# Score tiles by head instead of by residue: stacked high and low queries in the attention of a two-layer trunk

## The chip, the cores and the metric

The kernel runs on one core of a Trainium2 chip. The metric is the time of one execution on the device in microseconds (us); lower is better. Five engines matter: TensorE (PE; its weight loads are listed as PEld), VectorE (DVE), ScalarE (ACT), GpSimd (POOL) and SyncE (SP), which here issues the DMA loads.

## What is computed

A trunk of two layers for 256 tokens of width 1024: a mixture of three dilated causal attentions, a gated convolutional channel mixer, a gated linear attention, and the channel mixer again. The change is in the first of these. Cut to what matters:

```python
A_CONFIGS = ((128, 1), (512, 4), (2048, 16))     # window, dilation of groups 0, 1, 2

def dilated_branch(q, k, v, table, window, dilation):
    # query t attends t - j*dilation, j = 0..window/dilation, with a T5 bias
    ...
    s = jnp.einsum('bnqrhe,bnkrhe->bnrhqk', qb, kk).astype(jnp.float32) + bias[None, None, None]
    s = jnp.where(mask[None, :, None, None], s, NEG_INF)
    m = jnp.max(s, axis=-1, keepdims=True)
    p = jnp.exp(s - m)
    den = jnp.sum(p, axis=-1)
    o = jnp.einsum('bnrhqk,bnkrhe->bnqrhe', p, vv.astype(jnp.float32))
    ...

def dilated_mixture(h, w_in, w_out, rel_bias):
    qkv = (h @ w_in).reshape(B, S, A_GROUPS, 3, A_HEADS, A_HEAD_DIM)
    ...                                   # one branch for each group, joined by a softmax over their lse
    return o.reshape(B, S, A_WIDTH).astype(h.dtype) @ w_out
```

There are 16 heads of 64 channels. Because the branches are joined by a softmax of their log-sums, the kernel puts a query's scores of all three groups into one row and takes a single softmax over it: 256 scores of group 0 (dilation 1), and 64 each of groups 1 and 2, since with 256 tokens a query sees only keys of its own residue modulo 4 there (group 2's dilation of 16 is a mask within that residue).

## The kernel before

**Number format.** Most products are made of parts: a float32 value is split into a high part in a format of fewer bits that TensorE takes in one pass (`F32R`) and the rest, the low part, and `mm3` adds high·high, high·low and low·high. Plain `F32` products take several passes. Weights come in over SP in chunks of up to 2048 columns (`split`: tile `raw`, four buffers), ScalarE makes the high part `whi` (L172) and VectorE the low part `wlo` (L178), three buffers each.

**The attention loop** (L626) runs over eight pairs of heads; a pair fills the 128 partitions, head 0 in rows 0 to 63, head 1 in 64 to 127. For pair `u` it projects queries and keys of the groups 0, 1, 2 (`pqk`; three weight loads `wqk`), then values (`pv`; two loads `wv`, in the two rounds of `half`), then makes the scores (`scores`, L476) and the outputs of the pair before (`outputs`, L550). The turning of a pair's probabilities by TensorE (`turn`, L536) lies in the middle of the next pair's projections (L671, L678). Pairs 0 and 1 are projected together, from the first weights `w0` (L640 to L657). Six half chunks of the adaLN weights are loaded and multiplied in each pair from 2 on (`next_half`, L457).

**Evacuation** (`evacuate`, L576) of group 0: ScalarE writes the high part of the scaled queries (L586), VectorE their low part (L587), for each head; then ScalarE the high part of the keys and VectorE the low one (L591). The query tiles are zero where a row belongs to the other head: `q[0][a][:, r]` is, for a residue `r`, 128 rows by 2 x 64 columns with only the two diagonal blocks filled. GpSimd writes these zeros once, before the loop (L614).

**Score tiles.** There are four for a pair, one for each residue `r` modulo 4, 64 queries of head 0 in rows 0 to 63 and 64 of head 1 in rows 64 to 127. `shared` (L485) makes three products of 128 rows and 256 to 260 columns for each tile; `dilated` (L494) makes the small ones, 64 x 64 x 64 in plain `F32`: two groups by two heads for each tile. VectorE then adds the bias and takes the maximum (L510), with each query's bias row read backwards from tile `bias`; ScalarE takes the exponential (L529); VectorE divides by the sum and brings the keys into order by residue (`normalised`, L521 and L522).

**Bias rows.** `load_bias` (L364) fetches one tile for a pair with four DMAs from a small table in DRAM (`rows_d`), two buffers. In the loop it stands ahead of the pair's weight loads (L627).

**Order.** A scheduler puts each engine's instructions in a fixed order at compile time, by program order and its own model of time; an instruction that waits holds up everything behind it on its engine or queue. `tc.issue_after(x)` and the helper `behind(x)` only place an instruction after `x` on its engine. `behind(last_pv)` puts score products behind the last value product; the first tile's may come earlier (L503). PSUM tiles come from `bank`, with 2, 3 and 3 buffers of the tags p, s and t.

Of the kernel before, what the change touches and what calls it, by code (L numbers as in the profile page):

```python
# [18 lines left out]
P = 128  # L19
# [38 lines left out]
def trunk(ctx: ExitStack, tc: tile.TileContext, I, out):  # L58
# [305 lines left out]
    def load_bias(u):  # L364

        b = att.tile([P, KEYS + 3], F32, tag="bias", name="bias")
        r = rows_d[:, :]
        for hh in range(2):  # L370
            own, at = slice(CH * hh, CH * hh + CH), r.offset + (2 * u + hh) * NROW
            nc.sync.dma_start(b[own, 2 * CH :], bass.AP(r.tensor, at, [[4, CH], [1, T + 3]]))
            nc.sync.dma_start(b[own, 0 : 2 * CH].rearrange("p (g x) -> p g x", g=2),
                              bass.AP(r.tensor, at + 512, [[1, CH], [P, 2], [1, CH]]))
        return b[:, :]
# [100 lines left out]
    def scores(u, q, k, v, bias):  # L476
# [3 lines left out]
        prob = [att.tile([P, KEYS + 3], F32, tag="prob", name="prob", bufs=4) for _ in range(4)]  # L480

        def shared(s, r):
            n = T + r + r % 2
            for i, (a, b) in enumerate(((0, 0), (1, 0), (0, 1))):
                last = mm(s[:, 0:n], q[0][a][:, r].rearrange("p a b -> p (a b)"), k[0][b][:, 0:n], start=(i == 0), stop=(i == 2))  # L485
            return last

        def dilated(s, r):
            own = slice(CH * r, CH * r + CH)
            for g in (1, 2):  # L490
                at = T + r + CH * (g - 1)
                for hh in range(2):
                    e = slice(E * hh, E * hh + E)
                    last = mm(s[e, at : at + CH], q[g][e, own], k[g][e, own], start=True, stop=True)  # L494
            return last
# [3 lines left out]
        for tiles in ((0, 1, 2), (3,)) if u == 0 else (range(4),):  # L499
            s = {r: bank("s", "t" if r == 3 and u else "s") for r in tiles}  # L500
            for r in tiles:

                with behind(*(last_pv if r else last_t if u > 2 else [])):  # L503
                    last = shared(s[r], r)
            for r in tiles:
                with behind(last):
                    last = last_s[0] = dilated(s[r], r)
            for r in tiles:
# [41 lines left out]
    def outputs(u, of, pt, *after):  # L550
# [3 lines left out]
        with behind(*after):  # L554
            for n in range(2):
                for hh, e in enumerate(heads):
                    mm(grouped(po[e, :T]), v[n][:, e], pt[:, :, P * n + E * hh : P * n + E * hh + E], start=(n == 0), stop=False)
# [738 lines left out]
```

## Time and profile before

| | |
|---|---|
| runs | 769.24, 769.94, 769.95 us; median 769.94 |
| span of the profiled execution | 767.7 us; its time from outside is not shown |
| mean granted TensorE clock | 0.998 |
| HBM read | 182.59 MB, 239 GB/s over the span |
| `shared`, L485 | 96 products, 277 to 389 ns each by the trace |
| `dilated`, L494 | 128 products in 256 passes, 218 to 267 ns each by the trace |
| bias, maximum, L510 | 32 instructions, 546 to 561 ns each |
| bias loads, L372 and L373 | 32 DMAs, 450 to 1350 ns of SP each |

The profile is that of one execution. Times within it are us from the start of its span. Products overlap in the array, so how long one is said to take is more than what it adds; the distance from one start to the next tells that. In the rows of a timeline stand: start, duration, engine, line, operation, output<-inputs, tile shape and how many were merged; in brackets how long the engine idled before and who ended that.

### The profile page before, as it was taken

The page shows a single profiled execution, that of the slowest core. Times are in us where ns is not written, and L with a number is a line of the kernel's source. Part 1 is how long each engine was busy: PE and PEld are TensorE (multiplying, and loading weights), DVE is VectorE, ACT ScalarE, POOL GpSimd, SP SyncE. Part 2 cuts the span into 40 slices and gives each one's busy share as a digit, 9 for nine tenths or more (in the row PEclk, how much of TensorE's full clock was granted, in tenths as well). Part 3 has the DMA queues.
Part 4 walks back from the last instruction along what each step waited for, and adds up shares of the span by engine and source line. Part 5 has one row for each costly group of instructions (what it writes and reads, how often), then busy time and mean ns, then how long its engine had stood idle before and what let it go on. Part 6 is the DMA issues. An engine that isn't in the chain of part 4 may idle for free.

```text
span 767.7 us, 15963 instructions
## 1 busy us (share of the span) xinstructions
PE 759.3 (99%) x6430; PEld 739.0 (96%) x6430; DVE 640.6 (83%) x1160; ACT 485.5 (63%) x949; POOL 13.2 (2%) x28
## 2 busy tenths in 40 slices
PE   8999999999999999999999999999999999999997
PEld 6999999999999999999999998899999999999996
DVE  6998988888888869999999778797668899998552
ACT  6477566465646568776767556745767866666552
POOL 1000000000000010000000000000010000000100
PEclk9999999999999999999999999999999999999999
DMA  8989778787787347878646975875355777644531
GB/s 346 402 298 408 269 244 278 255 277 261 278 275 245 112 146 279 333 239 272 235 139 234 353 277 202 328 257 189 131 192 196 251 267 256 239 151 152 192 110 56
DMA packets 35208, 184.72 MB, mean 241 GB/s; under 512 B 6140, under 2 KB 7676, under 8 KB 21182
## 3 DMA queue, kind: packets, MB, share of 16 engines
q1 hardware_dynamic: 34752, 183.26, 67.7%
q8 instruction: 50, 0.82, 0.4%
q10 hardware_dynamic: 382, 0.45, 0.2%
q14 instruction: 24, 0.20, 0.1%
HBM read 182.59 MB, written 1.10 MB: 239 GB/s over the span
## 4 chain that ended last, share of the span: by engine, by line
PE 93%; DMA 3%; ACT 2%; DVE 2%; issue 0%; ACTq 0%
PE pab L200 10%; PE pab L199 10%; PE pab L201 10%; PE pqk L199 5%; PE pqk L201 5%; PE pqk L200 5%; PE pd L200 5%; PE pd L199 5%; PE pd L201 5%; PE pv L200 3%; PE pv L199 3%; PE pv L201 3%; DMA raw<-in_w 2%; PE py L199 2%; PE py L201 2%; PE py L200 2%
## 5 line engine op out<-in xcount | busy, mean ns | idle before, releaser
L172 ACT CAST whi<-raw 128x1024 fp32r<-128x1024 f32 (+4 forms) x270 | 243.7, 946 | 104.0 <-PE pab L200 37.2
L178 DVE TENSOR_TENSOR wlo<-raw,whi 128x1024 fp32r<-128x1024 f32 (+3 forms) x254 | 270.5, 1091 | 44.0 <-ACT whi L172 43.3
L200 PE MATMUL pab<-hlo,whi 128*128 128x256 f32 x672 | 184.6, 276 | 0.0
L201 PE MATMUL pab<-hhi,wlo 128*128 128x256 f32 x672 | 184.6, 276 | 0.0
L199 PE MATMUL pab<-hhi,whi 128*128 128x256 f32 x672 | 183.2, 277 | 0.0
L200 PEld LDWEIGHTS pab<-hlo,whi 128*128 128x128 f32 x672 | 126.0, 188 | 0.2
L201 PEld LDWEIGHTS pab<-hhi,wlo 128*128 128x128 f32 x672 | 126.1, 188 | 0.0
L199 PEld LDWEIGHTS pab<-hhi,whi 128*128 128x128 f32 x672 | 125.1, 188 | 0.1
L140 DVE CUSTOM_DVE_ANT_0 ada_raw<-ada_raw,c_bc 128x1024 f32<-128x1024 f32 x96 | 113.0, 1218 | 5.7 <-DMA ada_raw<-in_w_ada 4.2
L199 PE MATMUL pqk<-hhi,whi 128*128 128x256 f32 x356 | 98.0, 281 | 0.0
L200 PE MATMUL pqk<-hlo,whi 128*128 128x256 f32 x356 | 97.4, 279 | 0.0
L201 PE MATMUL pd<-ghi,wlo 128*128 128x256 f32 x352 | 96.9, 276 | 0.0
L200 PE MATMUL pd<-glo,whi 128*128 128x256 f32 x352 | 96.9, 276 | 0.0
L199 PE MATMUL pd<-ghi,whi 128*128 128x256 f32 x352 | 96.8, 276 | 0.0
L201 PE MATMUL pqk<-hhi,wlo 128*128 128x256 f32 x356 | 96.7, 279 | 0.0
L199 PEld LDWEIGHTS pqk<-hhi,whi 128*128 128x128 f32 x356 | 66.5, 188 | 0.2
L200 PEld LDWEIGHTS pqk<-hlo,whi 128*128 128x128 f32 x356 | 66.7, 188 | 0.0
L201 PEld LDWEIGHTS pqk<-hhi,wlo 128*128 128x128 f32 x356 | 65.9, 188 | 0.7 <-issue 0.7
L200 PEld LDWEIGHTS pd<-glo,whi 128*128 128x128 f32 x352 | 66.0, 188 | 0.0
L201 PEld LDWEIGHTS pd<-ghi,wlo 128*128 128x128 f32 x352 | 66.0, 188 | 0.0
L199 PEld LDWEIGHTS pd<-ghi,whi 128*128 128x128 f32 x352 | 65.9, 188 | 0.0
L852 ACT ACTIVATE r<-pab,small 128x256 f32<-128x256 f32 x86 | 47.4, 559 | 7.3 <-DVE r L855 6.9
(248 smaller groups left out, 1408.8 us busy)
## 6 DMA issues: line engine op xcount, KB each, us to landing
raw<-in_w_up SPq DMA_DIRECT2D x42, 1024.0 KB, 4.9
ada_raw<-in_w_ada SPq DMA_DIRECT2D x29, 1024.0 KB, 5.9
raw<-in_w_down SPq DMA_DIRECT2D x32, 704.0 KB, 4.1
ada_raw<-in_w_ada SPq DMA_DIRECT2D x38, 512.0 KB, 6.4
raw<-in_wqk SPq DMA_DIRECT2D x18, 1024.0 KB, 5.9
raw<-in_wv SPq DMA_DIRECT2D x14, 768.0 KB, 5.9
raw<-in_w SPq DMA_DIRECT2D x7, 960.0 KB, 6.4
raw<-in_w_out_a SPq DMA_DIRECT2D x4, 1024.0 KB, 6.6
```

What stands on the lines that cost most here:

```text
L140: i = nc.vector.tensor_tensor_reduce(w, w, c_bc, op0=ALU.mult, op1=ALU.add, scale=1.0, scalar=0.0, accum_out=dot,)
L172: copied[0] = nc.scalar.copy(hi[:, c], raw[:, c])
L178: last_lo[0] = nc.vector.tensor_tensor(lo[:, c], raw[:, c], hi[:, c].bitcast(F32), op=ALU.subtract)
L199: mm(ps, a[0], b[0], start=start, stop=False)
L200: mm(ps, a[0], b[1], start=False, stop=False)
L201: return mm(ps, a[1], b[0], start=False, stop=stop)
L852: nc.scalar.activation(r, u[:, :T], AF.Identity, scale=cw[2], bias=col(C_CB + 44 * l + f))
```

## The change

- A score tile now holds 128 queries of one head: tile `i` belongs to head `i % 2` and to the residues `2 * (i // 2)` and the next one, one above the other.
- The query tile `qs` holds for each head the high part in the head's own 64 rows and the low part in the other 64. The key tile `ks` holds for each head the high part of its keys in both halves. One product of 128 rows gives high·high + low·high (`shared`), one of the head's 64 rows gives high·low (`rest_of`): two for each tile instead of three.
- The products of a pair are ordered: those of 128 rows for all tiles, those of 64 rows, then the small ones. These go, for each half of the tiles and each group, through (head, residue) = (0,0), (1,1), (0,1), (1,0).
- In `evacuate` ScalarE writes both queries and the keys `kh` first, VectorE the low parts after, and GpSimd copies `kh` into `ks`, four copies of 64 x 256.
- Each head has its own bias tile, four DMAs each, so eight for a pair; single-buffered from pair 1 on (pair 0's stand in a tile of `pt`). From pair 2 on they are issued after the first value load of the pair.
- The zeros in the query tiles are no longer written. The outputs read the probabilities in the new layout. The first tile's products, too, come after the value products from pair 2 on.

The core of the diff:

```diff
@@ -363,16 +363,20 @@
     def load_bias(u):
-
-
-        b = att.tile([P, KEYS + 3], F32, tag="bias", name="bias")
+        both = []
         r = rows_d[:, :]
+        first = None if u else att.tile([P, 4, KEYS], F32, tag="pt", name="bias")
         for hh in range(2):
-            own, at = slice(CH * hh, CH * hh + CH), r.offset + (2 * u + hh) * NROW
-            nc.sync.dma_start(b[own, 2 * CH :], bass.AP(r.tensor, at, [[4, CH], [1, T + 3]]))
-            nc.sync.dma_start(b[own, 0 : 2 * CH].rearrange("p (g x) -> p g x", g=2),
-                              bass.AP(r.tensor, at + 512, [[1, CH], [P, 2], [1, CH]]))
-        return b[:, :]
+            b = (first[:, 2 * hh : 2 * hh + 2, :].rearrange("p a b -> p (a b)")[:, 0 : KEYS + 2] if u == 0
+                 else att.tile([P, KEYS + 2], F32, tag=f"bias{hh}", name="bias", bufs=1)[:, :])
+            at = r.offset + (2 * u + hh) * NROW
+            for x in range(2):
+                own = slice(CH * x, CH * x + CH)
+                nc.sync.dma_start(b[own, 2 * CH :], bass.AP(r.tensor, at + x, [[4, CH], [1, T + 2]]))
+                nc.sync.dma_start(b[own, 0 : 2 * CH].rearrange("p (g x) -> p g x", g=2),
+                                  bass.AP(r.tensor, at + 512, [[1, CH], [P, 2], [1, CH]]))
+            both.append(b)
+        return both
     sq = wspl.tile([P, 2048], F32, tag="wlo", name="sq").rearrange("p (k t) -> p k t", k=KT)
@@ -478,38 +482,51 @@
         m = tmp.tile([P, 16], F32, tag="m", name="m")
         prob = [att.tile([P, KEYS + 3], F32, tag="prob", name="prob", bufs=4) for _ in range(4)]
-
-        def shared(s, r):
-            n = T + r + r % 2
-            for i, (a, b) in enumerate(((0, 0), (1, 0), (0, 1))):
-                last = mm(s[:, 0:n], q[0][a][:, r].rearrange("p a b -> p (a b)"), k[0][b][:, 0:n], start=(i == 0), stop=(i == 2))
+        qs, (ks, kl) = q[0], k[0]
+
+        def width(i):
+            return T + 2 * (i // 2)
+
+        def shared(s, i):
+            hh, n = i % 2, width(i)
+            return mm(s[:, 0:n], qs[:, hh, P * (i // 2) : P * (i // 2) + P], ks[:, T * hh : T * hh + n], start=True, stop=False)
+
+        def rest_of(s, i):
+            hh, n = i % 2, width(i)
+            e = slice(E * hh, E * hh + E)
+            return mm(s[:, 0:n], qs[e, hh, P * (i // 2) : P * (i // 2) + P], kl[e, 0:n], start=False, stop=True)
+
+        def dilated(s, tiles):
+            for half in range(2):
+                for g in (1, 2):
+                    for hh, x in ((0, 0), (1, 1), (0, 1), (1, 0)):
+                        i = 2 * half + hh
+                        if i in tiles:
+                            e, own = slice(E * hh, E * hh + E), slice(CH * (2 * half + x), CH * (2 * half + x) + CH)
+                            at = width(i) + CH * (g - 1)
+                            last = mm(s[i][CH * x : CH * x + CH, at : at + CH], q[g][e, own], k[g][e, own], start=True, stop=True)
             return last
-        def dilated(s, r):
-            own = slice(CH * r, CH * r + CH)
-            for g in (1, 2):
-                at = T + r + CH * (g - 1)
-                for hh in range(2):
-                    e = slice(E * hh, E * hh + E)
-                    last = mm(s[e, at : at + CH], q[g][e, own], k[g][e, own], start=True, stop=True)
-            return last
-
         for tiles in ((0, 1, 2), (3,)) if u == 0 else (range(4),):
-            s = {r: bank("s", "t" if r == 3 and u else "s") for r in tiles}
-            for r in tiles:
-
-                with behind(*(last_pv if r else last_t if u > 2 else [])):
-                    last = shared(s[r], r)
-            for r in tiles:
+            s = {i: bank("s", "t" if i == 3 and u else "s") for i in tiles}
+            for i in tiles:
+                with behind(*(last_pv if i or u > 1 else [])):
+                    last = shared(s[i], i)
+            for i in tiles:
                 with behind(last):
-                    last = last_s[0] = dilated(s[r], r)
-            for r in tiles:
-                back = bass.AP(bias.tensor, bias.offset + KEYS - 1 + r, [bias.ap[0], [-1, KEYS + r]])
+                    ends = rest_of(s[i], i)
+            last = ends
+            with behind(last):
+                last_s[0] = dilated(s, tiles)
+            for i in tiles:
+                n = KEYS + 2 * (i // 2)
+                b = bias[i % 2]
+                back = bass.AP(b.tensor, b.offset + n - 1, [b.ap[0], [-1, n]])
                 nc.vector.tensor_tensor_reduce(
-                    prob[r][:, 0 : KEYS + r], s[r][:, 0 : KEYS + r], back,
-                    op0=ALU.add, op1=ALU.max, scale=1.0, scalar=-3e38, accum_out=m[:, r : r + 1],
+                    prob[i][:, 0:n], s[i][:, 0:n], back,
+                    op0=ALU.add, op1=ALU.max, scale=1.0, scalar=-3e38, accum_out=m[:, i : i + 1],
                 )
         pn = []
@@ -519,13 +536,13 @@
             f = m[:, 12 + r : 13 + r]
             pn.append(att.tile([P, KEYS], F32, tag="pn", name="pn", bufs=4))
             nc.vector.tensor_scalar(grouped(pn[r][:, 0:T]), by_residue(prob[r][:, 0:T]), f, None, op0=ALU.mult)
-            norms.append(nc.vector.tensor_scalar(pn[r][:, T:KEYS], prob[r][:, T + r : KEYS + r], f, None, op0=ALU.mult))
+            norms.append(nc.vector.tensor_scalar(pn[r][:, T:KEYS], prob[r][:, width(r) : KEYS + width(r) - T], f, None, op0=ALU.mult))
         for hh in range(2):
             rs = slice(2 * hh, 2 * hh + 2)
             nc.vector.tensor_scalar(m[:, 4:8][:, rs], m[:, 0:4][:, rs], -1.0, None, op0=ALU.mult)
             for r in (2 * hh, 2 * hh + 1):
-                c = prob[r][:, 0 : KEYS + r]
+                c = prob[r][:, 0 : KEYS + width(r) - T]
                 exps.append(nc.scalar.activation(c, c, AF.Exp, bias=m[:, 4 + r : 5 + r], accum_out=m[:, 8 + r : 9 + r]))
             nc.vector.reciprocal(m[:, 12:16][:, rs], m[:, 8:12][:, rs])
             for r in (2 * hh, 2 * hh + 1):
@@ -554,12 +571,12 @@
         with behind(*after):
             for n in range(2):
                 for hh, e in enumerate(heads):
-                    mm(grouped(po[e, :T]), v[n][:, e], pt[:, :, P * n + E * hh : P * n + E * hh + E], start=(n == 0), stop=False)
+                    mm(po[e, :T].rearrange("p (a b) -> p a b", a=2), v[n][:, e], pt[:, hh::2, P * n : P * n + P], start=(n == 0), stop=False)
             for r in range(4):
                 for hh, e in enumerate(heads):
                     at = P * (r % 2) + P + E * hh
                     last_po[0] = mm(po[e, CH * r : CH * r + CH], v[r // 2][:, at : at + E],
-                       pt[:, r, T + E * hh : T + E * hh + E], start=False, stop=(r == 3))
+                       pt[:, 2 * (r // 2) + hh, T + CH * (r % 2) : T + CH * (r % 2) + CH], start=False, stop=(r == 3))
         if u == 0:
             shift(att, 8)
         hi = att.tile([P, T], F32R, tag=f"ohi{u}", name="ohi", bufs=1)
@@ -580,16 +597,21 @@
         if g:
             evacuated[:] = nc.scalar.mul(q[g], pq, 0.125), nc.vector.tensor_copy(k[g], pk)
             return evacuated[1]
-        qh, ql = q[0]
-        for hh in range(2):
-            own = slice(E * hh, E * hh + E)
-            nc.scalar.mul(qh[own, :, hh, :], grouped(pq[own]), 0.125)
-            nc.vector.scalar_tensor_tensor(ql[own, :, hh, :], grouped(pq[own]), 0.125, qh[own, :, hh, :].bitcast(F32),
+        qs, (ks, kl, kh) = q[0], k[0]
+        k[0] = ks, kl
+        heads = [slice(E * hh, E * hh + E) for hh in range(2)]
+        for hh, own in enumerate(heads):
+            nc.scalar.mul(qs[own, hh, :], pq[own], 0.125)
+        high = nc.scalar.copy(as_tokens(kh[:, 0:T]), in_order(pk))
+        for hh, own in enumerate(heads):
+            nc.vector.scalar_tensor_tensor(qs[heads[1 - hh], hh, :], pq[own], 0.125, qs[own, hh, :].bitcast(F32),
                                            op0=ALU.mult, op1=ALU.subtract)
-        pk = in_order(pk)
-        kh, kl = (as_tokens(z[:, 0:T]) for z in k[0])
-        evacuated[:] = nc.scalar.copy(kh, pk), nc.vector.tensor_tensor(kl, pk, kh.bitcast(F32), op=ALU.subtract)
-        return evacuated[1]
+        low = nc.vector.tensor_tensor(as_tokens(kl[:, 0:T]), in_order(pk), as_tokens(kh[:, 0:T]).bitcast(F32), op=ALU.subtract)
+        for hh, own in enumerate(heads):
+            for to in heads:
+                nc.gpsimd.tensor_copy(ks[to, T * hh : T * hh + T], kh[own, 0:T])
+        evacuated[:] = high, low
+        return low
     def by_group(v, pv, n):
@@ -609,10 +631,11 @@
     for i in range(2):
         q_pair.append([])
         for j in range(2):
-            at, n = ((112, 2 * T + 112), (0, 2 * T + 16))[j] if i == 0 else (0, 2 * T)
+            at, n = ((112, 2 * T + 112), (0, 2 * T + 16))[j] if i == 0 else (0, 2 * T + 8 * j)
             z = att.tile([P, n], F32R, tag=f"q0{i}{j}", name="q", bufs=1)
-            nc.gpsimd.memset(z.bitcast(F32), 0.0)
-            q_pair[i].append(z[:, at : at + 2 * T].rearrange("p (r h c) -> p r h c", r=4, h=2))
+            if j:
+                nc.gpsimd.memset(z[:, 2 * T :].bitcast(F32), 0.0)
+            q_pair[i].append(z[:, at:] if j else z[:, at : at + 2 * T].rearrange("p (h c) -> p h c", h=2))
             if i == 0:
                 for s in range(2):
                     level[s].append(z[:, at + T * s : at + T * s + T])
@@ -624,14 +647,15 @@
                     nc.scalar.copy(a, b)
     for u in range(NPAIR):
-        with tc.issue_after(last_load[0].ins):
-            bias = load_bias(u)
+        if u < 2:
+            with tc.issue_after(last_load[0].ins):
+                bias = load_bias(u)
         place = u % 2 if u < 4 else 1
         if u == 0:
-            k_hi, k_lo = ([att.tile([P, T + 4], F32R, tag=f"k0{i}{j}", name="k", bufs=1) for j in range(2)] for i in range(2))
-            for z in k_hi + k_lo:
+            k_hi, k_lo = ([att.tile([P, T + 4 * (i or j)], F32R, tag=f"k0{i}{j}", name="k", bufs=1) for j in range(2)] for i in range(2))
+            for z in k_lo:
                 nc.gpsimd.memset(z[:, T:].bitcast(F32), 0.0)
-        q, k = [q_pair[place]], [[k_hi[place], k_lo[place]]]
+        q, k = [q_pair[place][0]], [(q_pair[place][1], k_lo[place], k_hi[place])]
         for g in (1, 2):
             q.append(att.tile([P, T], F32, tag=f"q{g}", name="q"))
             k.append(att.tile([P, T], F32, tag=f"k{g}", name="k"))
@@ -699,6 +723,9 @@
                     else:
                         hi = lo = ()
                     w = split(I["wv"][u - 1, half], 1536, after=(hi, ()), low=lo)
+                if u > 1 and half == 0:
+                    with tc.issue_after(last_load[0].ins):
+                        bias = load_bias(u)
                 for k4 in range(4):
                     kt = 4 * half + k4
                     wv = parts(w, 384 * k4, 384)
```

## The prediction

> **What bounds the kernel now.** I read the page's totals first, then the busy times over one period of the attention loop (the pairs repeat every 30.36 us; this row runs from the score products of pair 4 to those of pair 5), then TensorE's instructions in order of time.
>
> ```profile
> span 767.7 us, 15963 instructions
> PE 759.3 (99%) x6430; PEld 739.0 (96%) x6430; DVE 640.6 (83%) x1160; ACT 485.5 (63%) x949; POOL 13.2 (2%) x28
> ...
> 161.71:192.07 30.36, 30.36 (x273) 29.80 (x273) 26.09 (x53) 17.79 (x42) 0.00 (x0) 1.00 0.77 262
> ```
>
> In that row the length is followed by the busy time of PE, PEld, DVE, ACT and POOL, then the granted clock and the DMA share. TensorE is busy in every one of the 30.36 us, at full clock; VectorE has 4.3 us to spare, ScalarE 12.6, GpSimd is empty. So a pair lasts as long as its products, and what counts is when each group of them starts, not how long one is called busy (281 ns, while one starts every 118).
>
> ```profile
> 147.42 0.48 PE L485 MATMUL s<-k,q 128*128 128x256 f32 x2
> 147.75 0.28 PE L199 MATMUL pqk<-q,whi 128*128 128x256 f32 x1
> ...
> 153.27 0.28 PE L485 MATMUL s<-k,q 128*128 128x256 f32 x1
> 153.39 0.34 PE L199 MATMUL pv<-whi,hhi 128*128 128x384 f32 x1
> ...
> 161.71 1.24 PE L485 MATMUL s<-k,q 128*128 128x258 f32 x9
> 162.88 1.15 PE L494 MATMUL s<-k,q 64*64 64x64 f32 x32
> 163.96 1.08 PE L557 MATMUL po<-pt,v 128*64 128x256 f32 x8
> 164.87 0.64 PE L561 MATMUL po<-pt,v 128*64 128x64 f32 x16
> 165.43 0.39 PE L199 MATMUL pqk<-q,whi 128*128 128x256 f32 x1
> ```
>
> The twelve `shared` products of a pair are three early ones, used as fillers, and nine in a row. One costs 153.39 - 153.27 = 0.12 us (0.118 below, the spacing inside the nine); 9 x 0.118 = 1.06 of the 1.17 us to the first small product, so the change of tile shape costs 0.10. The 16 small products are float32 and show as 32 passes, in 1.08 us.
>
> How much runs side by side is read from these rows:
>
> ```profile
> 283.89 2.76 PE L329 MATMUL early<-early_x,raw 128*128 128x257 f32 x12
> 286.30 0.58 PE L199 MATMUL pab<-hhi,whi 128*128 128x256 f32 x2
> ...
> 507.11 0.28 PE L200 MATMUL pqk<-hlo,whi 128*128 128x256 f32 x1
> 507.32 0.48 PE L1040 MATMUL kv<-v,kdT 64*128 64x256 f32 x1
> 507.32 0.48 PE L1040 MATMUL kdt<-v,kdT 64*128 64x256 f32 x1
> 507.64 0.38 PE L1040 MATMUL kv<-v,kdT 64*128 64x256 f32 x1
> ...
> 507.85 0.59 PE L1040 MATMUL kv<-v,kdT 64*128 64x256 f32 x2
> 508.38 0.39 PE L201 MATMUL pqk<-hhi,wlo 128*128 128x256 f32 x1
> ```
>
> On the whole array twelve float32 passes of 257 columns take 2.41 us, 0.20 each. L557 has passes of the same length, yet eight of them take 0.91 us to L561: its two heads, in the two column halves of the array, run together. L1040 shows the same for row halves: `kv` and `kdt`, 64 rows each, start in the same instant, while the third product, on rows already used, takes its two passes alone (507.85 to 508.38). The small products run two at a time as well: 64 columns are a quarter of a pass, 0.05 us, and 32 of those one after the other would be 1.6 us, not 1.08. Two is what their order allows: each head has one quadrant of the array, rows and columns of its own half. L1040 also prices entering the 64-row shape: 0.21 from the last start before (0.10 above the usual 0.118), and 0.32 instead of 0.21 for the first pass, whose weights nothing hides: 0.10 + 0.10. For weights of 64 columns I take half of that, 0.05; of the 1.08 us then 0.05 is first weights, 0.10 the shape change out, and 0.93 the 16 slots, 0.058 each.
>
> **The change, part by part.** *Score products.* Four of 128 rows replace eight (high and low queries stacked, one high key under both), and four of 64 rows replace the other four. Tiles alternate heads, so the 64-row ones use alternate row halves and run in two slots, as L1040's did. Per pair, before: 12 x 0.118 + 0.10 (into 64x64) + 0.05 (first weights) + 0.93 + 0.10 (out) = 2.60. After: 4 x 0.118 = 0.47; 0.10 + 0.10 into 64 rows; 2 x 0.118 = 0.24; 0.10 + 0.05 into 64x64; the small ones; 0.10 out: 1.16 plus the small ones. If the 64-row products did not overlap: 0.24 more.
>
> *Small products.* Their count and size stay, but four in succession now lie in four different quadrants, two banks. No row of before has four at once. Bounds: 0.93 us (two at a time, as now) and 0.47 (8 slots). Column halves together (L557) and row halves together (L1040) both stand in the trace, so I take 0.47. The pair then costs 1.63 and saves 0.97; at 0.93 it saves 0.51. Pair 0 runs tiles 0 to 2 and then 3 apart, pays the extra shape change twice and has lone tiles with only two quadrants: by the same prices 0.43 saved (0.19 with two at a time). Sum: 7 x 0.97 + 0.43 = 7.2 us; with two at a time 3.8.
>
> The Trainium skill, page "TensorE: Matmul & The Clock Gate", section "Part 3: Packing small matmuls — row/col tiling", says that a weight load overlaps running products only where its row group differs. By it the quadrants of one head's rows would not overlap and the saving would stay at two at a time; L557's rows, same rows in both column halves, do not agree with it.
>
> *Fillers.* Tile 0's early products now wait for the value products. Behind them on PE stand L199 at 147.75 and 153.39, whose inputs are there (evacuation below ends 146.41), so they move up: nothing lost, 0.35 us a pair if not.
>
> *Evacuation, GpSimd, the wait for it.*
>
> ```profile
> 145.99 0.42 DVE L591 TENSOR_TENSOR k<-pqk,k 128x256 fp32r<-128x256 f32 x1 [0.44 <-ACT k L591]
> ...
> 62.48 0.42 DVE L591 TENSOR_TENSOR k<-pqk,k 128x256 fp32r<-128x256 f32 x1
> ...
> 64.66 0.64 PE L485 MATMUL s<-k,q 128*128 128x256 f32 x4
> ...
> L226 POOL TENSOR_TENSOR sqacc<-sq x4: 800/1066/1351, 276.6 to 716.5; 128x256 f32<-128x256 f32 x4
> ...
> L1022 POOL MEMSET a_t<- x4: 311/312/331, 464.5 to 526.3; 128x256 f32 x4
> ```
>
> Three ACT and three DVE instructions as before, now in two runs instead of alternating: at worst as late as today. Four GpSimd copies of 64x256 are new, a kind the trace lacks: between 0.31 us (a memset) and 1.35 (an addition with two inputs); with one input I take the middle, 0.7, 2.8 us for four (1.2 to 5.4). From 146.41 to the products at 161.71 there are 15 us: hidden in every pair from 2 on (uncovered: 2.8 us each). In pair 0 the keys are ready at 62.9 and PE wants them at 64.66; the high part is written about a microsecond before the low one and the first tile needs two copies, so 0, at most 2.4 once. What waits behind a late product is the whole of PE. The zero fills dropped at the start hide under the first loads: nothing.
>
> *Bias loads.* Eight instead of four per pair, single-buffered, and after pair 1 issued behind a value load instead of ahead of the pair.
>
> ```profile
> 122.67 4.12 SPq L166 DMA_DIRECT2D raw<-in_wv  x2
> ...
> 136.99 0.45 SPq L372 DMA_DIRECT2D bias<-rows_d  x1
> ...
> 136.40 0.55 DVE L510 CUSTOM_DVE_ANT_0 prob<-s,bias 128x387 f32<-128x387 f32 x1
> ...
> 164.18 0.56 DVE L510 CUSTOM_DVE_ANT_0 prob<-s,bias 128x384 f32<-128x384 f32 x1
> ...
> 140.96 1.56 ACT L172 CAST whi<-raw 128x768 fp32r<-128x768 f32 x2
> 146.97 1.58 ACT L172 CAST whi<-raw 128x768 fp32r<-128x768 f32 x2 [0.64 <-ACT pt L546]
> ...
> raw<-in_wv SPq DMA_DIRECT2D x12, 768.0 KB, 5.7
> bias<-rows_d SPq DMA_DIRECT2D x15, 64.8 KB, 4.7
> ```
>
> They cannot start before 136.95, when the last score tile has read the old rows; today's start at 136.99, for the same reason. Eight hold SP for 5.6 us (next rows) and the last lands 4.7 later: 147.3, 17 us ahead of the next reader at 164.18. Queued behind them on SP are the second value load, the adaLN halves and the next weights. Even if SP stopped right after the value load at 122.67 until 136.95, the second value load would be issued at 142.5 and land 5.7 later at 148.2, 1.2 after its cast at 146.97 today, for products that start halfway between 153.39 and 161.71, at 157.5. Cost 0; uncovered, some 5 us a pair.
>
> At the start they are not free:
>
> ```profile
> 49.35 0.52 SPq L372 DMA_DIRECT2D bias<-rows_d  x1
> ...
> 54.98 0.54 SPq L166 DMA_DIRECT2D raw<-in_wqk  x1
> ...
> 54.00:56.00 2.00, 2.00 (x17) 2.00 (x16) 2.00 (x5) 1.85 (x6) 0.00 (x0) 1.00 0.38 63
> 60.00:82.00 22.00, 22.00 (x193) 21.59 (x192) 18.83 (x41) 14.77 (x30) 0.00 (x0) 1.00 1.02 391
> ...
> 60.25 1.05 ACT L172 CAST whi<-raw 128x1024 fp32r<-128x1024 f32 x1 [0.79 <-DMA raw<-in_wqk]
> ...
> 67.83 0.28 PE L199 MATMUL pqk<-hhi,whi 128*128 128x256 f32 x1
> ```
>
> Eight loads hold SP from 49.35 to 54.98, with the DMA engines at 0.38 towards the end; sixteen hold the weights of pair 2 back 5.6 us more, just ahead of 22 us in which DMA is full. Those weights are cast from 60.25 and multiplied from 67.83, 7.6 us later, with two casts of 1.05 and VectorE's low half between: most of the delay is absorbed. Bounds 0 and 5.6; I take 0.7.
>
> **Sum.** -7.2 + 0.7 = -6.5 us, made on one execution whose span is 767.7; the 2.2 us between it and the runs' median of 769.94 stay as they are. Forecast: 769.9 - 6.5 = 763.4.
>
> **The rivals.** (1) The small products stay two at a time: 769.9 - 3.8 + 0.7 = 766.8. For it: nothing but pairs is in the trace; against it: L557 and L1040. (2) The start hands its whole delay to PE: 769.9 - 7.2 + 5.6 = 768.3. For it: DMA at 1.02 from 60 to 82; against it: the 7.6 us of lead. (3) The 64-row products do not overlap, and the small ones stay at two: 3.8 - 8 x 0.24 = 1.9 saved, 768.7 with the start; the change then hardly does what it says. Against it: L1040. (4) Slower: GpSimd's copies stop VectorE. DVE needs 26.1 us a pair, and a pair would last 29.4; if every copy holds it for its length, it becomes the bound from 3.3 us a pair on, 0.82 a copy. At 1.35 each DVE needs 31.5: 1.1 above today's 30.36, in six pairs 6.8: 776.7. For it: L226 on GpSimd varies from 0.80 to 1.35 us for one shape, as something waiting would; against it: it is a wait of GpSimd, not seen on DVE, and copies are lighter.
>
> The Trainium skill, page "SBUF — State Buffer", section "Who interferes with whom", has a rule for (4): a VectorE instruction with two SBUF inputs and a GpSimd instruction that reads SBUF exclude each other, and the later one stands for the whole of the first. No run yet shows which of the two is the later one here.
>
> **How the numbers follow.** Chances: forecast 0.58, (1) 0.22, (2) 0.08, (3) 0.04, (4) 0.08. A difference under 0.2% (1.5 us) cannot be told from none here. Faster: all of the forecast, nearly all of (1), half of (2) and (3): 0.84. Within 0.2%: their rests, 0.07. Slower: (4) and a little of (1) with (2): 0.09. The range runs from 761.6 (start free, and the new stage's 0.2 us of shape change and first weights partly hidden) to 768.7, which takes in (1), (2) and (3), and leaves (4) out; the forecast's own range is 761.6 to 765.
>
> **What would show it.** Right: periods of 29.4 us, the small products in about 0.5 us instead of 0.93, 64-row products starting in twos, PE without a gap in the loop. A period of 29.8 is rival (1); PE idle between 60 and 85 with a DMA as releaser is (2); DVE full in the period with GpSimd at over 3 us is (4). The forecast fails if any of PE's waits in the loop ends on GpSimd, the bias or VectorE.

## The result, and the profile after

The changed kernel takes 764.58 us (median of five runs, 764.08 to 767.97) where the kernel before, run beside it, takes 769.88: a ratio of 0.9942, 95% interval 0.9925 to 0.9959. That is 5.3 us less. Run again, unaltered, beside the last experiments, it took 764.18 (763.63 to 764.24), a ratio of 0.9923 (0.9909 to 0.9937). The forecast was 763.4.

The totals of the profiled execution (764.32 us), and the busy times of one period of the attention loop, from the output products of one pair to those of the next:

```profile
span 762.5 us, 15999 instructions
PE 754.1 (99%) x6398; PEld 731.6 (96%) x6398; DVE 642.6 (84%) x1160; ACT 485.8 (64%) x949; POOL 33.4 (4%) x56
...
161.16:190.55 29.39, 29.39 (x274) 28.70 (x270) 26.36 (x53) 17.91 (x42) 3.24 (x4) 1.00 0.82 284
```

The period is 29.39 instead of 30.36 us, TensorE is still busy in all of it, VectorE needs 0.27 more than the 26.09 of before, and GpSimd now has four instructions in 3.24 us. TensorE's rows ahead of such a period's end show where the 0.97 came from:

```profile
159.53 0.62 PE L492 MATMUL s<-q 128*128 128x256 f32 x4
160.08 0.50 PE L497 MATMUL s<-k,q 64*128 64x256 f32 x4
160.51 0.69 PE L507 MATMUL s<-k,q 64*64 64x64 f32 x32
161.14 1.08 PE L574 MATMUL po<-pt,v 128*64 128x256 f32 x8
162.05 0.64 PE L578 MATMUL po<-pt,v 128*64 128x64 f32 x16
```

From start to start, the score products take 0.55 + 0.43 + 0.63 = 1.61 us; L578 to the next stage is as before. The starts of the single passes say how many run together. These are ns from the first small pass of a pair (at 193.24 us before, at 189.90 us after); bars part the slots:

```
before  0 6 | 106 113 | 165 171 | 223 230 | 281 288 | ...  | 923 930                  (16 slots of 2)
after   0 6 13 20 | 107 113 120 126 | 165 171 178 185 | ... | 457 463 470 476        (8 slots of 4)
```

Four passes start 6 to 7 ns apart, and the next four 58 ns after them (107 ns after the first four): all four quadrants work at once. The Trainium skill, page "TensorE: Matmul & The Clock Gate", section "Part 3: Packing small matmuls — row/col tiling", lets a weight load overlap running products only where its row group differs. Two of these four share the rows of the other two, so the trace does not agree with that sentence; it does agree with the same section's table of measured speedups, where row and column tiles together gain more than either alone.

Cut into stretches by the first starts of single products, the three executions stand like this (us; the "pairs 3 to 7" run from pair 1's outputs to pair 6's; `py` are the products of the output projection, `early` and `pab` those of the channel mixer behind it):

| stretch | before | after | after, again | saving forecast |
|---|---|---|---|---|
| start of the span to the first product of `pqk` | 13.97 | 14.80 | 13.56 | 0 |
| to pair 1's outputs: scores of pairs 0, 1, 2 | 89.31 | 87.63 | 88.13 | 2.37, less 0.7 |
| pairs 3 to 7 | 151.77 | 146.98 | 146.98 | 4.85 |
| to `early`: pair 7's outputs, the projection | 26.68 | 27.65 | 27.65 | 0 |
| to the last product | 480.31 | 480.29 | 480.31 | 0 |
| last product to the end | 5.63 | 5.19 | 5.19 | 0 |
| span | 767.67 | 762.54 | 761.82 | 6.5 |

The loop gave 4.79 of 4.85. The first stretch differs between two executions of one program by 1.2 us, before anything that the change touches. The 480 us from `early` to the last product are the same. What is missing lies in two places: the start gave 1.2 to 1.7 instead of 2.37, and a loss of 0.97 between pair 7's outputs and `early` was in no term of the sum.

TensorE's rows show the latter. Before, the last outputs stood in one piece, L557's eight passes and L561's sixteen, 1.48 us to the next product:

```profile
270.48 1.08 PE L557 MATMUL po<-pt,v 128*64 128x256 f32 x8
271.40 0.64 PE L561 MATMUL po<-pt,v 128*64 128x64 f32 x16
271.96 0.39 PE L199 MATMUL py<-q,whi 128*128 128x256 f32 x1
```

In the changed kernel they do not:

```profile
263.06 0.65 PE L574 MATMUL po<-pt,v 128*64 128x256 f32 x2
263.63 0.39 PE L201 MATMUL py<-ohi,wlo 128*128 128x256 f32 x1
...
265.71 0.86 PE L574 MATMUL po<-pt,v 128*64 128x256 f32 x5
266.20 0.39 PE L578 MATMUL po<-pt,v 128*64 128x64 f32 x4
266.41 0.38 PE L574 MATMUL po<-pt,v 128*64 128x256 f32 x1
266.63 0.63 PE L578 MATMUL po<-pt,v 128*64 128x64 f32 x12
267.19 0.39 PE L199 MATMUL py<-q,whi 128*128 128x256 f32 x1
```

A score tile now belongs to one head. Head 0's first output product needs only tiles 0 and 2 (`pt[:, hh::2]`), so the scheduler places it ahead, alone, between projection products. It no longer shares the array with head 1's, and the shape changes twice more: 0.57 + 1.48 = 2.05 us, 0.57 more than before. The other 0.40 of the 0.97 lies in the `py` products of this stretch (192 of them, 23.14 instead of 22.74 us); some of it goes with the split too, as an experiment below shows. Pair 0's outputs are split in the same way, and tangled with pair 1's scores:

```profile
77.37 0.65 PE L574 MATMUL po<-pt,v 128*64 128x256 f32 x2
77.95 0.39 PE L492 MATMUL s<-q 128*128 128x258 f32 x1
78.27 0.50 PE L497 MATMUL s<-k,q 64*128 64x256 f32 x4
78.70 0.34 PE L507 MATMUL s<-k,q 64*64 64x64 f32 x8
78.97 0.86 PE L574 MATMUL po<-pt,v 128*64 128x256 f32 x5
```

In pairs 1 to 6 `behind(last_s)` puts the outputs after the scores, and they stay whole.

### The profile page after: what moved, and what is told of

The parts are those of the page before. It is cut to its first block, busy times and chain, and to the rows that moved or that the text cites. A ratio compares the mean times of both kernels' runs of the same rounds, so it can differ in the third digit from the quotient of the medians.

```text
span 762.5 us, 15999 instructions
## 1 busy us (share of the span) xinstructions
PE 754.1 (99%) x6398; PEld 731.6 (96%) x6398; DVE 642.6 (84%) x1160; ACT 485.8 (64%) x949; POOL 33.4 (4%) x56
## 4 chain that ended last, share of the span: by engine, by line
PE 92%; DVE 3%; ACT 2%; DMA 1%; issue 1%; ACTq 0%
PE pab L200 10%; PE pab L201 10%; PE pab L199 10%; PE pqk L199 5%; PE pqk L201 5%; PE pd L200 5%; PE pd L199 5%; PE pd L201 5%; PE pqk L200 5%; PE pv L199 4%; PE pv L200 4%; PE pv L201 4%; PE py L199 2%; PE py L201 2%; PE py L200 2%; PE t L561 1%
## 5 line engine op out<-in xcount | busy, mean ns | idle before, releaser
L178 DVE TENSOR_TENSOR wlo<-raw,whi 128x1024 fp32r<-128x1024 f32 (+3 forms) x254 | 270.6, 1091 | 40.8 <-ACT whi L172 39.9
L140 DVE CUSTOM_DVE_ANT_0 ada_raw<-ada_raw,c_bc 128x1024 f32<-128x1024 f32 x96 | 114.1, 1230 | 5.3 <-DMA ada_raw<-in_w_ada 5.2
```

The source lines that it names most:

```text
L140: i = nc.vector.tensor_tensor_reduce(w, w, c_bc, op0=ALU.mult, op1=ALU.add, scale=1.0, scalar=0.0, accum_out=dot,)
L178: last_lo[0] = nc.vector.tensor_tensor(lo[:, c], raw[:, c], hi[:, c].bitcast(F32), op=ALU.subtract)
```

## The experiments

All differ from the changed kernel only by the lines shown or named. The kernel before ran beside each group: 769.64 (the first four), 769.76 (the second four), 769.90 us (the last three).

### The order of the quadrants

```diff
-                for g in (1, 2):
-                    for hh, x in ((0, 0), (1, 1), (0, 1), (1, 0)):
+                for hh, x in ((0, 0), (1, 1), (0, 1), (1, 0)):
+                    for g in (1, 2):
```

> The two products of one quadrant follow each other directly instead of four quadrants in turn. Theory (passes are sent in the order written, so how many run side by side depends on how many different quadrants stand next to each other): the small products, 0.62 us from first to last start with the shape change out in the changed kernel, go to about 1.0 to 1.1 us, the period from 29.4 to about 29.85 us, the time 3 to 4 us above the changed kernel. Rival (the overlap belongs to the tiles' shape whatever the order): 0.62 us and no difference.

765.17 us (765.06 to 765.38). The period is 29.46 us; TensorE's rows:

```profile
160.95 0.76 PE L507 MATMUL s<-k,q 64*64 64x64 f32 x32
161.63 1.08 PE L574 MATMUL po<-pt,v 128*64 128x256 f32 x8
```

0.68 instead of 0.63 us from L507 to L574: the theory fell. The single starts now stand 13 ns apart (0, 14, 27, 40, then 108, 120, 134, 147), still four in each slot of 58 ns up to the last few. So it is not the succession of quadrants that gives the overlap; with four passes of one quadrant in a row, those of the other quadrants behind them still start in time. How far this goes is the next run:

```diff
-            for half in range(2):
-                for g in (1, 2):
-                    for hh, x in ((0, 0), (1, 1), (0, 1), (1, 0)):
+            for hh, x in ((0, 0), (0, 1), (1, 0), (1, 1)):
+                for half in range(2):
+                    for g in (1, 2):
```

> The small products are ordered quadrant by quadrant, eight passes of one before the next. Pairs of products in the same quadrant cost only 0.05 us a pair, so the engine must be able to take passes out of a queue for each quadrant, some way ahead. Theory (it looks only a few passes ahead): eight passes in a row block it, the passes run nearly one after the other, 32 x 0.058 = 1.9 us at most and about 1.5 us with the ends overlapping, 0.9 us a pair or 6 to 7 us in all above the changed kernel. Rival (it takes any of the 32): no difference beyond 0.5 us.

770.13 us (769.61 to 773.40), ratio 1.0009 (0.9997 to 1.0021): the whole gain of the change is gone.

```profile
166.29 1.54 PE L507 MATMUL s<-k,q 64*64 64x64 f32 x32
167.76 1.08 PE L574 MATMUL po<-pt,v 128*64 128x256 f32 x8
```

1.47 us, 0.84 more, and a period of 30.23. The theory held: four passes of a quadrant in succession do little harm, eight block the rest. The single starts of this pair show how. The passes that take 267 to 268 ns (the others take 218) start at 0, 289, 577 and 864 ns, and the starts between them fit four chains of eight passes. So these four are the first passes of the quadrants, and each starts 5 to 6 ns behind the fifth pass of the quadrant before (283, 571, 859), which then has three still to come. This is a reading of one trace: from the fifth pass in a row on, a quadrant holds up the next, whether the two share their rows (the first two) or not (the second and third). Runs of five to seven were not tried.

### The order by rows

```diff
             for i in tiles:
-                with behind(*(last_pv if i or u > 1 else [])):
+                with behind(*(last_pv if i or u > 1 else []), *([ends] if ends else [])):
                     last = shared(s[i], i)
-            for i in tiles:
                 with behind(last):
                     ends = rest_of(s[i], i)
```

(`ends` is None ahead of the loop.)

> The 64-row product of each tile stands right behind its 128-row product, so the four no longer share one change of shape and can't run two at a time. Theory (by the prediction's prices: 0.10 into 64 rows, 0.10 first weights, 0.118 each, 0.10 back): the eight products go from about 1.0 us to about 4 x 0.42 = 1.7 to 1.9, a pair to about 30.2, the time 5 to 7 us above the changed kernel, that is about equal to the kernel before. Rival (changes of shape between products of full width are hidden, only the lost overlap counts): 4 x 0.24 = 0.96 for the eight, 1 us or less above the changed kernel.

775.11 us (774.80 to 775.91), ratio 1.0064 (1.0048 to 1.0079): slower than before the change.

```profile
164.66 0.38 PE L492 MATMUL s<-q 128*128 128x256 f32 x1
164.98 0.38 PE L497 MATMUL s<-k,q 64*128 64x256 f32 x1
165.29 0.38 PE L492 MATMUL s<-q 128*128 128x258 f32 x1
165.60 0.39 PE L497 MATMUL s<-k,q 64*128 64x258 f32 x1
```

The rival fell, and the theory's price was too low. From the third on, each product starts 0.31 to 0.32 us after the one before: 0.118 and 0.195 for the change of shape, in both directions. The expectation had 0.20 into the 64-row shape, 0.10 of it for first weights, but only 0.10 out of it; the way back costs the same as the way in. The period is 30.81, 1.42 more, and the eight products alone take 1.41 more (2.39 against 0.98). Ordering the products by their rows is thus a necessary part of the change: without it the two products for a tile cost more than the three they replace.

### GpSimd's copies

Left out, or made twice, in pairs 2 to 7 (`times` is passed by the loop, as 0 or 2):

```diff
-                nc.gpsimd.tensor_copy(ks[to, T * hh : T * hh + T], kh[own, 0:T])
+                for _ in range(times):
+                    nc.gpsimd.tensor_copy(ks[to, T * hh : T * hh + T], kh[own, 0:T])
```

> GpSimd's four copies of the keys' high part are left out in pairs 2 to 7, whose score products then read the high keys of pairs 0 and 1. Theory (the copies lie in 15 us of slack and take nothing that sets the end): the period stays 29.4 us, the time within 0.5 us of the changed kernel. Rival (they hold up VectorE and through it PE): DVE's busy time per period falls by 1 us or more and the time by 2 us or more.

> Each of GpSimd's copies is made twice in pairs 2 to 7, some 3.4 us more of GpSimd per pair. Theory: no difference, because the second set still ends some 8 us ahead of the products. Rival (they hold up VectorE): the time rises by 2 us or more.

Left out: 765.01 us (764.20 to 767.54), not below the changed kernel. Twice: 765.81 (765.19 to 769.38). The busy times of the same three stretches (161.16 to 249.44 us), summed and as means of one stretch, first the changed kernel, then without copies, then with twice as many:

```profile
sum 88.28, PE 88.28 PEld 86.16 DVE 79.10 ACT 54.04 POOL 9.76; mean PE 29.43 PEld 28.72 DVE 26.37 ACT 18.01 POOL 3.25
```

```profile
sum 88.28, PE 88.28 PEld 86.20 DVE 78.65 ACT 54.17 POOL 0.00; mean PE 29.43 PEld 28.73 DVE 26.22 ACT 18.06 POOL 0.00
```

```profile
sum 88.28, PE 88.07 PEld 85.97 DVE 79.67 ACT 53.58 POOL 19.79; mean PE 29.36 PEld 28.66 DVE 26.55 ACT 17.86 POOL 6.60
```

Four copies cost VectorE 0.15 us a pair (26.37 - 26.22), four more 0.18. With 3 us to spare, next to nothing of it reaches TensorE at four copies (pairs 3 to 7 take 146.87 us without them, 146.98 with them); the theory held there. With eight, pairs 3 to 7 take 147.82 us: 0.10 to 0.17 more in four of the periods and 0.37 in the last, where TensorE waits 0.21 us, at 240.5, for VectorE's copy of a key. So "no difference" was too much for that run: the rival's mechanism is there, at a smaller size than its 2 us.

GpSimd's own row, and one of VectorE's beside it, show who pays for the contention:

```profile
L612 POOL CAST q<-k x32: 394/398/1492, 55.4 to 232.6; 64x256 fp32r<-64x256 f32 x32
```

```profile
174.57 1.41 DVE L140 CUSTOM_DVE_ANT_0 ada_raw<-ada_raw,c_bc 128x1024 f32<-128x1024 f32 x1
```

The first row gives minimum, median and maximum in ns. In pairs 3 to 7 the four copies of a pair take 0.92 to 0.98, 0.40, 0.40 and 1.48 to 1.49 us. The two short ones run beside VectorE's L607 and L609, each of which reads one of its inputs from PSUM (`pqk`); the first runs beside a weight split (L178) and the last beside L140, which both read two tiles in SBUF. The next L140 behind the last copy takes 1.41 us, against 1.22 without copies: that is what VectorE loses. The Trainium skill, page "SBUF — State Buffer", section "Who interferes with whom", says that a VectorE instruction with two SBUF inputs and a GpSimd instruction that reads SBUF exclude each other; the trace agrees with it (0.40 us beside instructions with one input in SBUF, up to 1.49 beside those with two), and here it is mostly GpSimd that waits.

### The outputs of both heads together

```diff
-                for hh, e in enumerate(heads):
-                    mm(po[e, :T].rearrange("p (a b) -> p a b", a=2), v[n][:, e], pt[:, hh::2, P * n : P * n + P], start=(n == 0), stop=False)
+                for hh in (1, 0):
+                    e = heads[hh]
+                    with behind(*([] if hh else [second])):
+                        second = mm(po[e, :T].rearrange("p (a b) -> p a b", a=2), v[n][:, e], pt[:, hh::2, P * n : P * n + P], start=(n == 0), stop=False)
```

> Head 1's output product is issued ahead of head 0's, so the products of both heads stay together in pairs 0 and 7, where the changed kernel issues head 0's alone some time ahead. Theory (each of these two separations loses the overlap of the two column halves and pays extra changes of shape): the 25 output passes go from 2.05 to about 1.48 us at the start and at the end, the scores of pair 1 and the next products join without the extra changes, and the time falls 0.8 to 1.5 us below the changed kernel. Rival (nothing of what is missing from the forecast lies there): the time within 0.4 us of the changed kernel.

763.89 us (762.93 to 766.99). The end got 0.75 of its 0.97 back: from pair 6's outputs to `early` 26.89 instead of 27.65. The other 0.22 stays, in `py` products that start a little further apart (22.96 against 22.74 us for the 192); its cause is open. The start got nothing: from the first `pqk` to pair 1's outputs 88.11, where the change alone has 87.63 and 88.13, though the outputs stand in one piece:

```profile
78.28 1.08 PE L576 MATMUL po<-pt,v 128*64 128x256 f32 x8
79.20 0.64 PE L580 MATMUL po<-pt,v 128*64 128x64 f32 x16
79.76 0.39 PE L492 MATMUL s<-q 128*128 128x258 f32 x1
```

The longest wait of TensorE between 45 and 300 us (the row gives us in all, times, the longest), and VectorE's rows at it, tell why:

```profile
PE pv L199 <- DVE k L600: 0.7, 1, 0.7
```

```profile
86.43 1.81 DVE L178 TENSOR_TENSOR wlo<-raw,whi 128x768 fp32r<-128x768 f32 x2
88.17 0.15 DVE L543 TENSOR_SCALAR m<-m 128x2 f32<-128x2 f32 x1
88.24 0.94 DVE L178 TENSOR_TENSOR wlo<-raw,whi 128x768 fp32r<-128x768 f32 x1
89.11 0.15 DVE L543 TENSOR_SCALAR m<-m 128x2 f32<-128x2 f32 x1
89.18 0.94 DVE L178 TENSOR_TENSOR wlo<-raw,whi 128x768 fp32r<-128x768 f32 x1
90.05 0.41 DVE L600 COPY k<-pqk 128x256 f32<-128x256 f32 x1
```

VectorE is busy without a gap from 80 to 90 us, and the copy that frees the bank for the next value products stands behind four weight splits. A faster TensorE only reaches this wait earlier.

### The bias loads at the start

One bias for pairs 0 and 1 (pair 1's scores then have pair 0's bias):

```diff
-        if u < 2:
+        if u < 1:
             with tc.issue_after(last_load[0].ins):
                 bias = load_bias(u)
```

> Pair 1 uses pair 0's bias; eight of the sixteen bias loads at the start are left out. Theory (the start takes at most the 0.7 us that the prediction gave it, and what else is lost there has other causes): the weights of pair 2 are issued at about 55 us as in the kernel before, and the time is 0 to 0.7 us below the changed kernel. Rival (the bias loads delay the start through the DMA queue): 1 to 4 us below it, and the runs scatter less.

765.52 us (764.77 to 769.75), not below the changed kernel, and the scatter is no smaller. The weights of pair 2 are issued at 54.85 instead of 60.85 us, so the delay is gone and nothing is gained: the rival fell. (The profiled execution, 767.73 us, is one with a late start: its first `pqk` is at 17.38 us.)

The other way, pair 1's loads on GpSimd's queue, with the outputs together:

```diff
-                nc.sync.dma_start(b[own, 2 * CH :], bass.AP(r.tensor, at + x, [[4, CH], [1, T + 2]]))
+                (nc.gpsimd if u == 1 else nc.sync).dma_start(b[own, 2 * CH :], bass.AP(r.tensor, at + x, [[4, CH], [1, T + 2]]))
```

(and the same for the second load)

> The outputs together as in the run before, and pair 1's eight bias loads issued from GpSimd's queue instead of SyncE's. Theory: the weights of pair 2 are issued at about 55 us, the time is that of the run with outputs together less 0 to 0.7 us, about 763. Rival (GpSimd's DMA issue is slow and late, and pair 1's scores wait for the bias): slower than outputs together alone.

766.44 us (765.89 to 767.69): 2.5 us slower than the outputs together. The trace's waits from 50 to 100 us:

```profile
POOL bias L375 <- DMA rows_d<-rows: 48.5, 1, 48.5
```

GpSimd stands 48.5 us at the first of these loads until the rows are in DRAM. The time is the rival's, but no wait of this stretch ends on the bias. The scheduler's order at the start changed with it too (pair 0's first score product moves from 57 to 65 us), and TensorE now waits 1.8 us for ScalarE's values near 60 us and 2.1 for VectorE's probabilities at 102, so this run does not say what costs the 2.5 us.

### VectorE's pace at the start

The last three ran side by side on one chip: the changed kernel, the outputs together, and the outputs together with one copy moved from VectorE to ScalarE:

```diff
-    def evacuate(q, k, g, pq, pk):
+    def evacuate(q, k, g, pq, pk, copy=nc.vector.tensor_copy):
...
-            evacuated[:] = nc.scalar.mul(q[g], pq, 0.125), nc.vector.tensor_copy(k[g], pk)
+            evacuated[:] = nc.scalar.mul(q[g], pq, 0.125), copy(k[g], pk)
...
-                done = evacuate(q, k, g, pq, pk)
+                done = evacuate(q, k, g, pq, pk, *([nc.scalar.copy] if (u, g) == (2, 1) else []))
```

> The changed kernel unaltered, beside the next two on one chip. Both theories: 764.3 to 765.2 us. The first matrix product on the first row loaded starts at 2.2 us in a usual execution and at 3.0 in its first profile; at 2.2 the span is not shorter by the whole 0.8, since the start afterwards waits for other things.

> The run with the outputs together once more, for a direct comparison. Theory (the split of pair 7's outputs costs 0.76 us, that of pair 0's 0.57, but at the start a wait of 0.7 us for VectorE's copy of a key takes its place): 0.7 us below the changed kernel, and the wait of PE on DVE's line 600 at about 90 us is there again. Rival (the difference was scatter): the same time.

> The outputs together, and the one copy of a key that PE waited 0.7 us for at 90 us (pair 2, second group, behind three weight splits on a full VectorE) is made on ScalarE, which has 2.2 us idle there. Theory (VectorE sets the pace of the start, not the bias loads): the wait goes, pair 1's outputs start 0.5 to 0.7 us earlier, the time falls 0.4 to 0.7 us below the run with outputs together alone, to about 763.2. Rival (the DMA, full from 60 to 90 us, sets the pace): PE waits elsewhere instead, within 0.2 us of it.

| kernel | median, range (us) | first `pqk` to pair 1's outputs | pair 6's outputs to `early` |
|---|---|---|---|
| changed | 764.18 (763.63 to 764.24) | 88.13 | 27.65 |
| outputs together | 764.58 (763.10 to 766.76) | 88.64 | 26.89 |
| and the key copy on ScalarE | 763.21 (762.44 to 763.41) | 87.23 | 26.89 |

The outputs together alone are no better here: the rival holds for the time as a whole. The trace shows what takes back the gain at the end: the wait for the copy is there again, 1.0 us this time. (The profiled execution also starts 0.89 us later than that of the changed kernel and has a slower stretch of 0.47, see the last section.)

```profile
PE pv L199 <- DVE k L600: 1.0, 1, 1.0
PE pqk L201 <- DVE wlo L178: 0.3, 1, 0.3
PE pv L199 <- ACT v L626: 0.3, 1, 0.3
```

With the copy on ScalarE, only one wait of the products is left:

```profile
PE pv L199 <- ACT v L626: 0.3, 1, 0.3
```

Counted from the first `pqk`, pair 1's outputs come 1.4 us earlier than with the outputs together alone, and all runs lie below all runs of the changed kernel; the ranges of the two kernels with the outputs together overlap. The DMA is as full as before it (1.01 from 70 to 90 us in this trace too), so it was VectorE and not the DMA that set this pace: the theory held. This version is the fastest: 0.9909 of the time before (0.9895 to 0.9924), 6.7 us.

## Why the prediction was right, and where not

- **A saving of 0.97 us a pair: right.** 30.36 - 29.39 = 0.97, with the terms as they were costed: 1.61 us for the new score products against the 1.63 worked out. Over pairs 3 to 7 it is 4.79 of 4.85. 0.55 stands for 0.47 + 0.10, 0.43 for 0.10 + 0.24 + 0.10, 0.63 for 0.05 + 0.47 + 0.10.
- **Small products four at a time: right, by a reason that was too narrow.** They run in 8 slots of 58 ns. The prediction put it down to four in succession lying in four quadrants; the order within the four doesn't matter (0.05 us a pair), their being in four quadrants does, as long as no quadrant has eight passes in a row (0.84 us a pair). Rival (1) is out.
- **64-row products in twos: right.** Two start 3 to 4 ns apart and the next two 0.22 us after them; rival (3) is out.
- **Fillers, evacuation, GpSimd at nothing: right.** The copies were priced at 0.7 us each and average 0.70, which is luck: half of them take 0.40, the others up to 1.49. They take 0.15 us of VectorE a pair, where rival (4) needed 3.3. No wait of TensorE in the profile ends on GpSimd.
- **The start's debit of 0.7: the size was about right, the mechanism was not.** In place of 2.37 us the start gave 1.68 in one execution and 1.18 in another, a debit of 0.7 to 1.2; that this is near 0.7 is luck. The prediction put it to the bias loads ("sixteen hold the weights of pair 2 back 5.6 us more"), and leaving out half of them gives nothing back. What the traces show in its place is pair 0's outputs, split (0.57), and short waits for a full VectorE and a full ScalarE; when the outputs are joined the wait for VectorE takes the place of the split, and only with that copy moved does the start give 2.08 of the 2.37. The prediction also said that no wait of TensorE in the loop would end on VectorE; one of a weight load does, 0.2 us at 91.0 us, for a copy of a key.
- **The outputs' new layout at no cost: wrong, 0.97 us.** This is the step that failed: the prediction's sum has no term for it, and its part on the change doesn't take up that the outputs read the probabilities in another layout. The products are the same, but what each of them waits for is not, and with that their place in the scheduler's order. Joining them gave back 0.75 at the end; the cause of the other 0.22 is open.

The sum of 6.5 thus stands against 5.1 of span in the first profile: 7.2 forecast, less 0.06 in the loop, less 0.7 at the start, less 0.97 at the end, less 0.83 for a late start of this one execution, plus 0.44 behind the last product. Nothing in the change explains the 0.44: every profile with the change has 5.2 to 5.3 us there, and the one profile of before 5.63.

## What to carry to other kernels

Small products spread over four quadrants of the array took 8 slots here where two quadrants took 16, as long as no quadrant had more than four passes in a row. Products of other row counts should be gathered by shape, since each change between 128 and 64 rows costs 0.195 us here in either direction. When a layout changes, list anew what each reader waits for: a product that becomes ready earlier may be placed earlier, apart from the partner with which it shared the array. And where a second engine is full, a saving on the first only moves the wait; look at what stands ahead of the copy that frees the next bank.

## What the runs showed that was not expected

- **Executions of one program start differently.** The first matrix product starts at 2.2 to 2.4 us in some profiles and at 3.0 to 3.1 in others, behind the first row's load, and the first `pqk` at 13.6 to 17.5. The two profiles with 17.4 and 17.5 (one bias; quadrant by quadrant) are of runs 2.2 and 3.3 us above their kernels' medians, so such starts account for part of the scatter.
- **A slower stretch that the granted clock doesn't show.** In three of the four profiles with the outputs together, products of `pab` start 118 ns apart instead of 113 for some 13 us behind the second `early`, from 576 us on, and in one of them behind the first `early` too. Each costs 0.48 us. The row of the fastest kernel for that time has the clock at 1.00 (the number ahead of the DMA share). One other profile has such a stretch (the products by tile); the changed kernel's two, and the fourth with the outputs together (bias loads on GpSimd), have none. The cause stays open.

```profile
580.00:590.00 10.00, 10.00 (x87) 10.00 (x86) 8.47 (x14) 7.18 (x15) 0.00 (x0) 1.00 0.63 216
```
